# A three-layer float32 network on one core: norm weights spread by one transfer, fewer weight splits on GpSimd, and weights split earlier at the experts' end

## The chip, the core and the metric

The kernel runs on one core of a Trainium2 chip. The core has TensorE (PE, matrix products), VectorE (DVE), ScalarE (ACT), GpSimd (POOL) and SyncE (SP, which issues transfers); each takes its instructions in one fixed order and stands still while the next one waits. Transfers run on 16 DMA engines. The metric is the device time of one execution in microseconds; lower is better.

## The reference, cut to what matters

256 tokens of width 1024 go through two layers and then a second block, all in float32:

```
for i in (0, 1):
    h = gdn_mixer(x, ...) if i == 0 else s5_mixer(x, ...)    # gated delta rule / state space
    x = layer_norm(ALPHA * x + h, ln_g[i, 0], ln_b[i, 0])
    f = swiglu(x, ...) if i == 0 else moe_swiglu(x, ...)     # dense, d_ff 2816 / 8 experts, top 2
    x = layer_norm(ALPHA * x + f, ln_g[i, 1], ln_b[i, 1])
x = x + mixer(rmsnorm(x, norm_mix_g))                        # pooling and neighbourhood attention
x = x + mlp(rmsnorm(x, norm_mlp_g))                          # up, squared relu, down
out = rmsnorm(x, final_g)

layer_norm: (x - mean) * rsqrt(var + 1e-5) * g + b           # g and b have 1024 entries
```

Each weight is read from memory once.

## The kernel before

**Weights.** Every weight matrix is stored in the order of use. `load` (L310) fetches chunks of 1 MB on SyncE's queue into raw buffers `wr` (three of them, and a few more, `wx`, in the experts). A chunk holds two *pieces* of 128x1024. Each piece becomes two parts, so that the products keep float32's accuracy: `wh`, a copy by ScalarE (L290), and `wl`, the difference raw minus `wh` (L292). A product is made of three matmuls (L336 to L338: high by high, low by high, high by low). There are five buffers each for `wh` and `wl`, so at most five pieces are prepared at once; `wget` hands out the next piece and prepares those up to `self.ahead` (three) further on.

**Which engine makes `wl`.** VectorE does, except for the pieces that a stage names with `pool_splits`, which GpSimd does. Before the change GpSimd does 32 of them: 14 in the first mixer, 8 in the feed-forward, 3 in the state-space layer, 2 at the experts' end and 5 at the start of the second block.

**Norms.** A tile is 128 tokens, so there are two. `ln_part` (L848) adds the branch to the residual and takes statistics, `ln_finish` makes the deviation's inverse (L857, L365, L368, L372) and applies the norm: L868 subtracts the mean and multiplies by the gain, L870 multiplies by the inverse deviation and adds the offset. Both read `gb`, where gain and offset lie on all 128 partitions. `to_features` (L830) transposes the result on TensorE, L835 and L836 split it into two parts. `ln_rows` fills `gb` for each of the four norms of the layers, `gains` fills `gr` for the second block's: small transfers of one row each to one partition on GpSimd's queue, then one GpSimd instruction per row that spreads it over the partitions.

**Order.** The code is written in one order; side work is spawned as generators that advance as pieces of weights pass. A scheduler then decides in which order each engine gets its instructions; `issue_after` holds one instruction behind another of the same engine. So the change of one line can move neighbours too.

**The experts' end.** The last expert's second product fills two banks `pdn`; each result is split into `y1` (ScalarE) and `y2` (VectorE), scattered back to the tokens by a product `psc`, and added to `acc` (L1707). A norm with its gains follows, L1799 multiplies by the second block's gain, and TensorE transposes the outcome (`ptr`). Meanwhile TensorE runs 20 products that nothing reads (`warm`, L260).

**The first mixer's inverse.** `inverse` runs 15 dependent steps on VectorE (L610 multiply, L612 reduce), sends the result to memory (`d`) and fetches it back in another layout (`td`, eight loads on L618, half of them on SyncE's queue), and L627 goes on with it.

Of the kernel before, what the change touches and what calls it, by code (L numbers as in the profile page):

```python
# [16 lines left out]
ALU = mybir.AluOpType  # L17
# [34 lines left out]


def _cols(w, nb):
    """[K, F] -> [128, F/128/nb, nb, K/128, 128] flat per partition."""
    k, f = w.shape
    return w.reshape(k // 128, 128, f // 128, 128).transpose(1, 2, 0, 3).reshape(128, -1)


def _rows(w):  # L60
    """[K, N] -> [128, N/512, K/128, 512] flat per partition."""
    k, n = w.shape
    return w.reshape(k // 128, 128, n // 512, 512).transpose(1, 2, 0, 3).reshape(128, -1)


def _first(w):
    """The first 512 columns by rows, the others by columns."""
# [3 lines left out]
def _vec(v):  # L71
    """[K] -> [128, K/128]."""
    return v.reshape(-1, 128).T
# [5 lines left out]
def _consts():  # L79
    """Masks and index tables that the shapes alone fix, in three groups."""  # L80
# [33 lines left out]
def pack(i):  # L114
    """Device arrays from the inputs: transposes, slices and static gathers only."""
# [13 lines left out]
    # small vectors, features on partitions  # L129
# [10 lines left out]
    # FFN: w1 and w3 block by block  # L140
# [6 lines left out]
    # S5  # L147
# [14 lines left out]
    # experts  # L162
# [9 lines left out]
    # second block  # L172
# [31 lines left out]
class Kern:  # L204
# [16 lines left out]
    # -- small helpers --  # L221
# [15 lines left out]
    def spawn(self, gen, lag=0):  # L237
        """Work that runs beside the weights; it yields how many pieces of weights to let pass."""
# [15 lines left out]
    def warm(self, n):  # L254
        """Products that nothing reads, where TensorE would wait so long that its clock falls to half."""
# [7 lines left out]
    # -- weights: float32 from memory, split exactly into two float32r parts --  # L263
    def schedule(self, ap, chunks, at=0):
        """Append chunks of one weight array (lists of widths of pieces) to the order of loads."""
# [9 lines left out]
    def pool_splits(self, *ks):  # L275
        """Which of the pieces to come GpSimd splits."""
        self.on_pool.update(len(self.pieces) + k for k in ks)

    def prep(self, upto):
        """Load and split pieces as far as this one, or as the buffers reach."""  # L280
        nc = self.nc
        first = self.n_got - 1 if self.held is None else self.held
        while self.n_split <= min(upto, first + BUFS - 1, len(self.pieces) - 1):
# [5 lines left out]
            with self.tc.issue_after(self.after.ins) if self.after else nullcontext():  # L289
                nc.scalar.activation(hi[:, :w], src, AF.Copy)  # L290
# [5 lines left out]
    def load(self, c, upto=None):  # L296
        """Loads as far as the buffers reach while chunk c is in use."""
# [16 lines left out]
    def wget(self):  # L314
        """The next piece of weights (hi, lo); loads and splits run ahead of it."""
# [4 lines left out]
    def hold(self):  # L320
        """Keep the pieces from here on until they are let go."""
# [6 lines left out]
    def split(self, x1, x2, src):  # L328
        """x1 + x2 = src, both float32r."""
# [10 lines left out]
    def colblock(self, out):  # L340
        """out[f, tok] = sum over features of the next 128-column block of weights."""
# [6 lines left out]
    def rsqrt(self, pool, y, v, n):  # L348
        """y = v ** -0.5 for small tiles [128, n], Newton from an integer start."""
# [9 lines left out]
    def rsqrt1(self, y, v, mul, eps):  # L359
        """y = (mul v + eps) ** -0.5 for a few columns: a start from the table, then one Newton step."""  # L360
# [13 lines left out]
    # ------------------------------------------------------------ first layer  # L374
# [29 lines left out]
    def router(self, P):  # L404
        """The router's weights for rows that wait for their layer norm: gain in, mean out; the offset's share with the bias."""
# [15 lines left out]
    def plan_gdn(self):  # L421
        self.pool_splits(2, 5, *range(16, 24), 25, 27, 29, 31)
# [5 lines left out]
    def gdn(self):  # L428
# [4 lines left out]
        # chunks of weights that come while the buffers are full of the first ones, in the room of later matrices  # L433
# [13 lines left out]
        def gates():  # L447
            """beta and the log decays, tokens on partitions."""
# [24 lines left out]
            # log1p(e2) = ln(w) e2 / (w - 1), and e2 where w is 1  # L473
# [20 lines left out]
        def until(what, *hs):  # L494
            """Let weights pass until what comes first in the program has been put there."""
# [3 lines left out]
        # decay between every pair of tokens: segments (s0,t0) (s0,t1) (s1,t1)  # L499
# [17 lines left out]
        def project(out, base):  # L517
            """The next 128 channels: causal taps."""
# [1518 lines left out]
```

## Time and profile before

| | |
|---|---|
| median of 3 runs | 1309.83 us (1307.24 to 1312.06) |
| span of the profiled execution | 1305.7 us |
| TensorE busy | 1230.1 us, 94% of the span |
| VectorE busy | 1037.9 us, 79% |
| ScalarE busy | 732.7 us, 56% |
| GpSimd busy | 353.4 us, 27% |
| weights and other data read | 260.79 MB, 201 GB/s over the span |

The span runs from the first to the last instruction of one profiled execution; no separate time of that execution is listed, and the median of the runs shown lies 4.1 us above the span. Busy means that an instruction is in the engine; an instruction that is held by another engine's access counts as busy too, so its length has to be compared with that of its like. TensorE's busy time includes stretches at the lower of its two clock levels (1.2 instead of 2.4 GHz, shown as a granted clock of 0.50), where the same product takes about twice as long.

### The profile page before, as it was taken

To read this page: it belongs to the slowest core of one execution; us is meant where nothing else is said; L and a number is where in the kernel's file an instruction comes from. 1 tells how busy PE (TensorE), PEld (TensorE's weight loads), DVE (VectorE), ACT (ScalarE), POOL (GpSimd) and SP (SyncE) were. 2 spreads that over 40 slices of the span, in tenths; PEclk is the share of its full clock that TensorE was granted. 3 is DMA by queue.
4 is the path that set the end of the run, shared out by engine and by line. 5 is a ranking of instruction groups with operands and counts; after the bars stand their busy time and mean duration, and the time that the engine had idled before them with its cause. 6 is when DMAs were issued, how large, how long until landed. Compare 5 with 4: busy or idle time off the path is not lost. (4 is left out here: it accounts for less than half of the span.)

```text
span 1305.7 us, 19759 instructions
## 1 busy us (share of the span) xinstructions
PE 1230.1 (94%) x7579; PEld 1065.1 (82%) x7579; DVE 1037.9 (79%) x1487; ACT 732.7 (56%) x1086; POOL 353.4 (27%) x321
## 2 busy tenths in 40 slices
PE   8989997998997989899999999999999789999997
PEld 7989876997996777667888888888877677899886
DVE  6677879999865898779998989999988775766553
ACT  6635444442443544448777777767767455655442
POOL 2362014249996656223000000000003371000000
PEclk9989999899998999999999999999999899999999
DMA  8343214453651501136999889899987543455551
GB/s 324 130 138 120 85 65 151 159 188 134 227 194 65 178 33 65 57 130 217 344 343 338 326 322 373 300 333 373 335 302 293 180 151 130 166 190 187 183 189 54
DMA packets 44437, 263.46 MB, mean 202 GB/s; under 512 B 9136, under 2 KB 9536, under 8 KB 18096
## 3 DMA queue, kind: packets, MB, share of 16 engines
q1 hardware_dynamic: 40320, 257.12, 55.2%
q10 hardware_dynamic: 3472, 4.42, 1.0%
q8 instruction: 62, 1.02, 0.3%
q0 software_dynamic: 544, 0.58, 0.1%
q14 instruction: 39, 0.32, 0.1%
HBM read 260.79 MB, written 1.31 MB: 201 GB/s over the span
## 5 line engine op out<-in xcount | busy, mean ns | idle before, releaser
L292 DVE TENSOR_TENSOR wl<-wr,wh 128x1024 fp32r<-128x1024 f32 (+1 forms) x361 | 441.0, 1240 | 125.9 <-ACT wh L290 123.8
L290 ACT ACTIVATE wh<-wr 128x1024 fp32r<-128x1024 f32 (+2 forms) x390 | 391.1, 1025 | 234.4 <-PE po L338 85.8
L338 PE MATMUL pup<-wh,xg 128*128 128x512 f32 (+1 forms) x384 | 145.2, 378 | 2.7 <-PEq L1668 2.4
L337 PE MATMUL pup<-wl,xg 128*128 128x512 f32 (+1 forms) x384 | 146.3, 381 | 0.3 <-DVE wl L292 0.2
L336 PE MATMUL pup<-wh,xg 128*128 128x512 f32 (+1 forms) x384 | 145.9, 380 | 0.0
L292 DVE TENSOR_TENSOR wl<-wx,wh 128x1024 fp32r<-128x1024 f32 (+1 forms) x110 | 122.4, 1146 | 10.5 <-ACT wh L290 8.8
L290 ACT ACTIVATE wh<-wx 128x1024 fp32r<-128x1024 f32 (+1 forms) x112 | 105.0, 980 | 9.9 <-PE pup L338 5.9
L292 POOL TENSOR_TENSOR wl<-wr,wh 128x1024 fp32r<-128x1024 f32 x29 | 76.6, 2656 | 108.3 <-ACT wh L290 77.4
L338 PE MATMUL p<-x,wl 128*128 128x256 f32 x320 | 92.3, 288 | 5.5 <-DVE wl L292 5.3
L336 PE MATMUL p<-x,wh 128*128 128x256 f32 x320 | 91.7, 287 | 0.0
L337 PE MATMUL p<-x,wh 128*128 128x256 f32 x320 | 91.4, 286 | 0.0
L337 PEld LDWEIGHTS pup<-wl,xg 128*128 128x128 f32 x384 | 72.5, 189 | 14.3 <-DVE wl L292 4.0
L338 PEld LDWEIGHTS pup<-wh,xg 128*128 128x128 f32 x384 | 72.6, 189 | 14.1 <-issue 2.8
L336 PEld LDWEIGHTS pup<-wh,xg 128*128 128x128 f32 x384 | 72.8, 190 | 10.9 <-issue 0.2
L337 PE MATMUL pdn<-wl,eh 128*128 128x512 f32 x176 | 69.9, 397 | 0.0
L336 PE MATMUL pdn<-wh,eh 128*128 128x512 f32 x176 | 69.8, 397 | 0.0
L338 PE MATMUL pdn<-wh,eh 128*128 128x512 f32 x176 | 69.5, 395 | 0.0
L338 PEld LDWEIGHTS p<-x,wl 128*128 128x128 f32 x320 | 62.3, 195 | 7.0 <-DVE wl L292 6.9
L336 PE MATMUL pm<-x,wh 128*128 128x256 f32 x224 | 63.5, 283 | 0.0
L338 PE MATMUL pm<-x,wl 128*128 128x256 f32 x224 | 63.4, 283 | 0.0
L337 PE MATMUL pm<-x,wh 128*128 128x256 f32 x224 | 63.4, 283 | 0.0
L336 PEld LDWEIGHTS p<-x,wh 128*128 128x128 f32 x320 | 62.4, 195 | 0.6 <-ACT s L995 0.4
(565 smaller groups left out, 3123.2 us busy)
## 6 DMA issues: line engine op xcount, KB each, us to landing
wr<-w_e SPq DMA_DIRECT2D x59, 1024.0 KB, 6.7
wx<-w_e SPq DMA_DIRECT2D x37, 1024.0 KB, 6.7
wr<-w_f SPq DMA_DIRECT2D x33, 1024.0 KB, 4.8
wr<-w_e SPq DMA_DIRECT2D x29, 768.0 KB, 5.8
wr<-w_up SPq DMA_DIRECT2D x16, 1024.0 KB, 4.9
wr<-w_dn SPq DMA_DIRECT2D x16, 1024.0 KB, 4.9
wx<-w_e SPq DMA_DIRECT2D x19, 768.0 KB, 6.0
wr<-w_glu SPq DMA_DIRECT2D x8, 1024.0 KB, 4.7
```

Of the source, the lines that this page charges most:

```text
L290: nc.scalar.activation(hi[:, :w], src, AF.Copy)
L292: self.los[self.n_split] = eng.tensor_tensor(lo[:, :w], src, hi[:, :w], op=ALU.subtract)
L336: mm(out, lhsT=l1, rhs=r1, start=start, stop=False)
L337: mm(out, lhsT=l1, rhs=r2, start=False, stop=False)
L338: self.mm = mm(out, lhsT=l2, rhs=r1, start=False, stop=stop)
```

## The change

1. **Norm weights.** `ln_rows` and `gains` call a new function `spread`. It issues one transfer on ScalarE's queue that reads the rows once for each partition and writes all 128 (1 MB for two rows, 0.5 MB for one). The small transfers and the GpSimd spreading instructions are gone; there are six such fills.
2. **GpSimd's splits.** The lists of `pool_splits` are shortened. In the instructions as built GpSimd makes 12 differences instead of 32; the other 20 (six in the first mixer, seven in the feed-forward, three in the state-space layer, one at the experts' end, three at the second block's start) are VectorE's.
3. **The experts' end.** Before the last piece of the last expert is taken, `self.ahead` becomes four, so that one more piece of the second block is prepared; the last `y1` is issued behind the last `wh` made so far, and `y2` behind the last `wl`.

Comments and docstrings are removed too, so line numbers differ between the two files (L815 and L817 become L821; L868 and L870 become L870 and L872).

```diff
-                nc.scalar.activation(hi[:, :w], src, AF.Copy)
+                self.hi = nc.scalar.activation(hi[:, :w], src, AF.Copy)
...
     def plan_gdn(self):
-        self.pool_splits(2, 5, *range(16, 24), 25, 27, 29, 31)
+        self.pool_splits(2, 5, 16, 17, 25, 27, 29, 31)
...
     def ln_rows(self, i, pool, tag, rr=True):
         self.gb = pool.tile([128, 2, D], F32, tag=tag, name="gb")
-        for k in range(2):
-            self.nc.gpsimd.dma_start(self.gb[0:1, k, :], self.a["lnrow"][2 * i + k:2 * i + k + 1, :])
-        for k in range(2):
-            self.nc.gpsimd.partition_broadcast(self.gb[:, k, :], self.gb[0:1, k, :])
+        self.spread(self.gb, self.a["lnrow"][2 * i:2 * i + 2, :])
...
+    def spread(self, out, rows):
+        n = rows.shape[0]
+        self.nc.scalar.dma_start(out[:, :n, :], rows.partition_broadcast(128))
...
     def gains(self, i, n, pool, tag):
         g = pool.tile([128, 2, D], F32, tag=tag, name="gr")
-        for k in range(n):
-            self.nc.gpsimd.dma_start(g[0:1, k, :], self.a["rmsrow"][i + k:i + k + 1, :])
-        for k in range(n):
-            self.nc.gpsimd.partition_broadcast(g[:, k, :], g[0:1, k, :])
+        self.spread(g, self.a["rmsrow"][i:i + n, :])
...
     def plan_ffn(self):
-        self.pool_splits(0, 1, 2, 4, 6, 8, 10, 12)
+        self.pool_splits(0)
...
     def plan_s5(self):
-        self.pool_splits(0, 1, 2)
...
     def plan_moe(self):
-        self.pool_splits(36 * NE - 3, 36 * NE - 1)
+        self.pool_splits(36 * NE - 3)
...
                 for k0 in range(0, EB, 2):
+                    if (e, n) == (NE - 1, 1) and k0 + 2 >= EB:
+                        self.ahead = BUFS - 1
                     hi, lo = self.wget()
...
-                self.split(y1, y2, py)
+                with tc.issue_after(self.hi.ins) if (e, n) == (NE - 1, 1) else nullcontext():
+                    nc.scalar.activation(y1, py, AF.Copy)
+                with tc.issue_after(self.los[self.n_split - 1].ins) if (e, n) == (NE - 1, 1) else nullcontext():
+                    TT(y2, py, y1, op=ALU.subtract)
...
         self.drain()
+        self.ahead = BUFS - MO["a"]
...
     def plan_second(self):
-        self.pool_splits(0, 1, 2, 3, 4)
+        self.pool_splits(0, 2)
```

**The first place: SyncE's queue in the first mixer.** `w_go` are the mixer's output weights, `td` the inverse's result on its way back. Before:

```order
L310 DMA wr<-w_z 128x2048
L310 DMA wr<-w_q 128x2048 x4
L605 DMA d_152<-nd_146 16x16x16 x4
L310 DMA wr<-w_v 128x2048 x4
L618 DMA td<-d_153 16x16x16 x4
L310 DMA wr<-w_go 128x2048 x4
L310 DMA wr<-w_f 128x2048 x33
```

and in the changed kernel:

```order
L310 DMA wr<-w_z 128x2048
L310 DMA wr<-w_q 128x2048 x4
L605 DMA d_152<-nd_146 16x16x16 x4
L310 DMA wr<-w_v 128x2048 x4
L310 DMA wr<-w_go 128x2048
L618 DMA td<-d_153 16x16x16 x4
L310 DMA wr<-w_go 128x2048 x3
L310 DMA wr<-w_f 128x2048 x33
```

The first chunk of `w_go` now stands ahead of the four loads of `td`.

**The second place: VectorE between the feed-forward and the state-space layer.** The rows begin at the first tile's norm (`lnr` holds the sums, `gb` the gain and offset, `x` the normed rows; `x_71<-ptr` is the low part of the transposed rows). Before:

```order
L868 SCALAR_TENSOR_TENSOR lnr<-lnr,lnmv,gb 128x512 x2
L848 SCALAR_TENSOR_TENSOR lnr<-x,po 128x512
L368 SCALAR_TENSOR_TENSOR rs_4585<-lnrs,rs_4583 128x1
L849 BN_STATS lnst<-lnr 128x6
L372 SCALAR_TENSOR_TENSOR lnrs<-rs_4585,lnrs 128x1
L870 SCALAR_TENSOR_TENSOR x<-lnr,lnrs,gb 128x512 x2
L848 SCALAR_TENSOR_TENSOR lnr<-x,po 128x512
L292 TENSOR_TENSOR wl<-wr,wh 128x1024
L836 TENSOR_TENSOR x_71<-ptr,x_70 128x4x128 x2
L849 BN_STATS lnst<-lnr 128x6
L292 TENSOR_TENSOR wl<-wr,wh 128x1024
L857 BN_AGGR lnmv<-lnst 128x2
```

and in the changed kernel:

```order
L870 SCALAR_TENSOR_TENSOR lnr<-lnr,lnmv,gb 128x512 x2
L850 SCALAR_TENSOR_TENSOR lnr<-x,po 128x512
L368 SCALAR_TENSOR_TENSOR rs_4579<-lnrs,rs_4577 128x1
L851 BN_STATS lnst<-lnr 128x6
L372 SCALAR_TENSOR_TENSOR lnrs<-rs_4579,lnrs 128x1
L292 TENSOR_TENSOR wl<-wr,wh 128x1024
L872 SCALAR_TENSOR_TENSOR x<-lnr,lnrs,gb 128x512 x2
L850 SCALAR_TENSOR_TENSOR lnr<-x,po 128x512
L292 TENSOR_TENSOR wl<-wr,wh 128x1024
L838 TENSOR_TENSOR x_71<-ptr,x_70 128x4x128 x2
L851 BN_STATS lnst<-lnr 128x6
L292 TENSOR_TENSOR wl<-wr,wh 128x1024
```

A split of weights (L292) now stands ahead of the normed rows `x`, a second one ahead of the transposed rows' low part, and a third directly behind the second tile's statistics.

**The third place: VectorE at the experts' end.** `y` from `pdn` is the low part of the last result, `acc<-psc` the last sum, `lnst` the norm's statistics. Before:

```order
L331 TENSOR_TENSOR y_14731<-pdn,y_14730 128x512
L292 TENSOR_TENSOR wl<-wx,wh 128x1024
L1632 SCALAR_TENSOR_TENSOR acc<-psc,rgate,acc 128x512 x2
L292 TENSOR_TENSOR wl<-wx,wh 128x1024
L1698 BN_STATS lnst<-acc 128x6 x2
L331 TENSOR_TENSOR y_14803<-pdn,y_14802 128x512
L1707 SCALAR_TENSOR_TENSOR acc<-psc,rgate,acc 128x512
L1708 BN_STATS lnst<-acc 128x6
L857 BN_AGGR lnmv<-lnst 128x2
L365 TENSOR_SCALAR rs_14850<-lnmv 128x1
```

and in the changed kernel:

```order
L1685 TENSOR_TENSOR y_14719<-pdn,y_14718 128x512
L292 TENSOR_TENSOR wl<-wx,wh 128x1024
L1630 SCALAR_TENSOR_TENSOR acc<-psc,rgate,acc 128x512 x2
L292 TENSOR_TENSOR wl<-wx,wh 128x1024
L292 TENSOR_TENSOR wl<-wx,wh 128x512
L1703 BN_STATS lnst<-acc 128x6 x2
L292 TENSOR_TENSOR wl<-wr,wh 128x1024 x2
L1685 TENSOR_TENSOR y_14795<-pdn,y_14794 128x512
L292 TENSOR_TENSOR wl<-wr,wh 128x1024
L1712 SCALAR_TENSOR_TENSOR acc<-psc,rgate,acc 128x512
L1713 BN_STATS lnst<-acc 128x6
L859 BN_AGGR lnmv<-lnst 128x2
```

Ahead of the last `y` there are three more splits (one of 128x512), and a fourth stands between it and the last sum.

## Rows read from the trace of the kernel before

**Rows 1.** The page's first two parts: span; busy time, share, instructions of each engine.
```profile
span 1305.7 us, 19759 instructions
...
PE 1230.1 (94%) x7579; PEld 1065.1 (82%) x7579; DVE 1037.9 (79%) x1487; ACT 732.7 (56%) x1086; POOL 353.4 (27%) x321
```

**Rows 2.** Waits of TensorE: who waits for whom, us in all, times, longest.
```profile
PE ptn L954 <- DVE s L981: 5.8, 1, 5.8
```

**Rows 3.** Windows: busy us of PE, PEld, DVE, ACT, POOL; clock; DMA share; GB/s.
```profile
80.00:100.00 20.00, 16.69 (x117) 16.48 (x116) 19.45 (x45) 8.76 (x16) 8.55 (x4) 0.83 0.46 159
225.00:325.00 100.00, 90.14 (x652) 85.88 (x653) 99.67 (x169) 38.40 (x54) 54.86 (x51) 0.97 0.45 153
405.00:425.00 20.00, 11.01 (x51) 9.92 (x50) 11.67 (x17) 6.47 (x9) 7.51 (x7) 0.74 0.00 0
425.00:435.00 10.00, 7.48 (x34) 5.17 (x34) 9.67 (x11) 1.14 (x3) 7.94 (x5) 1.00 0.59 211
600.00:1000.00 400.00, 397.27 (x1888) 333.95 (x1887) 362.21 (x386) 296.03 (x358) 7.60 (x4) 1.00 0.91 335
1010.00:1030.00 20.00, 13.13 (x50) 9.10 (x50) 19.10 (x31) 7.42 (x16) 8.67 (x4) 0.74 0.30 105
```

**Rows 4.** The page's costliest groups: the weight splits of VectorE.
```profile
L292 DVE TENSOR_TENSOR wl<-wr,wh 128x1024 fp32r<-128x1024 f32 (+1 forms) x361 | 441.0, 1240 | 125.9 <-ACT wh L290 123.8
```

**Rows 5.** Line 610 by source; then timelines of GpSimd and SyncE in the first mixer.
```profile
L610 DVE TENSOR_TENSOR pr<-tt,nd x15: 172/410/2144, 79.5 to 98.7; 128x1 f32<-128x1 f32 x1, 128x4 f32<-128x4 f32 x1, 128x9 f32<-128x9 f32 x1, 128x16 f32<-128x16 f32 x1
...
90.17 2.36 POOL L292 TENSOR_TENSOR wl<-wr,wh 128x1024 fp32r<-128x1024 f32 x1 [3.67 <-ACT wh L290]
...
102.87 5.35 SPq L618 DMA_DIRECT2D td<-d  x4
...
109.47 0.35 SPq L310 DMA_DIRECT2D wr<-w_go  x1
```

**Rows 6.** Timeline of VectorE from the first mixer's end into the feed-forward.
```profile
198.83 3.53 DVE L870 SCALAR_TENSOR_TENSOR x<-lnr,lnrs,gb 128x512 f32<-128x512 f32 x2
...
220.93 5.20 DVE L1134 TENSOR_SCALAR SS<-SS 128x64 f32<-128x64 f32 x5
...
232.23 3.39 DVE L292 TENSOR_TENSOR wl<-wr,wh 128x1024 fp32r<-128x1024 f32 x1
```

**Rows 7.** Timelines between feed-forward and state-space layer: GpSimd, then VectorE, then TensorE.
```profile
412.54 2.48 POOL L817 PARTITION_BROADCAST gb<-gb  x2 [5.82 <-issue]
...
413.87 2.21 DVE L868 SCALAR_TENSOR_TENSOR lnr<-lnr,lnmv,gb 128x512 f32<-128x512 f32 x2 [8.05 <-POOL gb L817]
...
427.84 2.32 DVE L368 SCALAR_TENSOR_TENSOR rs<-lnrs,rs 128x1 f32<-128x1 f32 x1
...
418.37 1.12 PE L830 MATMUL ptr<-cg,x 128*128 128x128 f32 x4 [8.99 <-DVE x L870]
...
434.06 1.32 PE L830 MATMUL ptr<-cg,x 128*128 128x128 f32 x8 [1.07 <-DVE x L870]
```

**Rows 8.** Timelines at the experts' end: GpSimd, then VectorE, then TensorE.
```profile
1006.60 12.07 POOL L292 TENSOR_TENSOR wl<-wr,wh 128x1024 fp32r<-128x1024 f32 x5
...
1008.64 0.69 DVE L331 TENSOR_TENSOR y<-pdn,y 128x512 fp32r<-128x512 f32 x1 [1.98 <-ACT y L330]
...
1009.92 0.75 DVE L1707 SCALAR_TENSOR_TENSOR acc<-psc,rgate,acc 128x512 f32<-128x512 f32 x1 [0.59 <-PE psc L1625]
...
1014.09 2.29 DVE L368 SCALAR_TENSOR_TENSOR rs<-lnrs,rs 128x1 f32<-128x1 f32 x1
...
1026.38 0.21 DVE L368 SCALAR_TENSOR_TENSOR rs<-lnrs,rs 128x1 f32<-128x1 f32 x1
...
1021.42 1.94 PE L830 MATMUL ptr<-cg,xn 128*128 128x128 f32 x8 [6.87 <-DVE xn L1799]
...
1030.72 1.03 PE L830 MATMUL ptr<-cg,xn 128*128 128x128 f32 x8
```

**Rows 9.** The page's transfers: a 1 MB weight chunk, KB, us to landing.
```profile
wr<-w_f SPq DMA_DIRECT2D x33, 1024.0 KB, 4.8
```

## The prediction

> **What bounds the kernel now.** The page's first two parts come first: TensorE is busy for 94% of 1305.7 us, VectorE for 79%, GpSimd for 27% [rows 1]. So about 75 us at most can be won from TensorE's idle time, and the question is where that time lies. The windows answer it. In the experts (600 to 1000 us) TensorE works 397.27 of 400 us; nothing is to be had there. From 405 to 425 us it works 11.01 of 20, from 1010 to 1030 us 13.13 of 20, from 80 to 100 us 16.69 of 20, and in the feed-forward's first 100 us 90.14, while VectorE is full there (99.67) [rows 3]. In the three short windows the granted clock is 0.74, 0.74 and 0.83, so TensorE spent part of them at 1.2 GHz after it had stood idle. The waits and the timelines then say who was waited for. At 418.37 us `ptr` had waited 8.99 us for the normed rows, whose norm stood 8.05 us for `gb` from GpSimd [rows 7]. At 1021.42 us `ptr` had waited 6.87 us for `xn` [rows 8]. In the feed-forward `ptn` waited 5.8 us for `s` [rows 2].
>
> The second thing to see is a length. The same small operation of VectorE, line 368, takes 2.32 us at 427.84, 2.29 us at 1014.09 and 0.21 us at 1026.38 [rows 7, 8]. The long ones lie beside a GpSimd split (five of those fill 1006.60 to 1018.67, 2.41 us each [rows 8]), the short one beside none. So a split on GpSimd isn't free for VectorE: one that meets a VectorE operation of this kind costs it about 2.1 us. On VectorE the split itself costs 1.24 us [rows 4].
>
> **Part by part.** The sum goes by the place where TensorE waits, in us gained.
>
> *The feed-forward's end.* GpSimd spreads `gb` at 412.54 to 415.02, late because its own work precedes it; line 868 starts at 413.87 and had been idle for 8.05, so it could have begun at 405.82 [rows 7]. The new transfer reads its rows long before: it stands in ScalarE's queue ahead of the last groups of the feed-forward, and a 1 MB transfer takes 4.8 us to land [rows 9]. From line 868's start to `ptr` are 4.50 us (413.87 to 418.37). In the new order one split, 1.24 us, stands ahead of `x`. So `ptr` comes at 405.82 + 4.50 + 1.24 = 411.6, 6.8 us earlier. What follows shrinks too. The second tile's `ptr` stands at 434.06, 15.7 us behind the first. Of those, TensorE idled 2.5 (425 to 435: 7.48 of 10 busy). A clock of 0.74 over 20 us means 10.4 us at half rate; 9 of the 20 were idle, so about 5 fell on work and cost 2.5 [rows 3]. Without both it is 10.7 us; the three splits that VectorE takes over here (3.7 us) about match the holds that go. I take 11: second `ptr` at 422.6, a gain of 11.5. Bounds: 7 if the 15.7 us stay as they are, 13 if the split ahead of `x` falls into idle time as well.
>
> *The experts' end.* Three more splits, one of them half size, now stand ahead of the last `y`, a fourth ahead of the last sum: 3.5 x 1.24 = 4.3 us. VectorE idled 1.98 and 0.59 us just there, so 1.7 us remain, and the sum starts at 1011.6 instead of 1009.92 [rows 8]. From it to `ptr` were 11.50 us. Three operations in between (868, 368, 372) are held by GpSimd's five splits, 2.1 us each by the row of 368: 6.2 us. GpSimd now has two of those five, which end about 1011.4 (1006.60 + 2 x 2.41), before these operations. That makes 11.5 - 6.2 = 5.3 us and `ptr` at 1016.9, 4.5 earlier. The low clock (again 10.4 us of 20, some 5 on work) may add up to 2.5 us, but the second tile's chain behind it doesn't shrink alike; I take 5, bounds 2 (all four splits on the path) and 8 (low clock gone, splits hidden).
>
> *The first mixer.* Six splits add 7.4 us to VectorE between 74 and 100 us. Four of line 610's steps take about 2 us (longest 2.144) where the shortest takes 0.172 [rows 5]: about 7.4 us are given back. VectorE was busy 19.45 of 20 us and stays so. TensorE's 3.3 us of idle time and the low clock (0.83: 6.8 us at half rate, 3.4 lost) are the most to be won, 6.7. Against it stands SyncE's queue: the first `w_go` chunk, issued at 109.47, now stands ahead of `td`, whose loads went out from 102.87 to 108.22 [rows 5]. `w_go` waits for a raw buffer that the last splits of queries free; if it waits as before, `td` starts 6.9 us later and ends at least 3 us later, and the inverse with it. I take 1, bounds -5 and 6.7.
>
> *Into the feed-forward.* Seven splits are 8.7 us more on a VectorE that is full. Three rows show what goes: two operations of line 870 took 3.53, where one of that shape takes 0.75; five tiny ones of line 1134 took 5.20 (0.21 each would be 1); a split took 3.39 instead of 1.24 [rows 6, 8, 4]. Together 2.0 + 4.2 + 2.15 = 8.4. I take 0. Bounds: 9, if the wait for `s` (5.8) goes and the low clock with it (0.97 over 100 us: 3 lost), and -4, if half of the holds would have been in VectorE's idle time.
>
> *What costs nothing.* Six issues on ScalarE at about 0.35 us (as SyncE's `w_go` [rows 5]); ScalarE is busy 56%, and its slack covers them (2 us if not). In the experts two fills put 1.5 MB on the transfer engines, 4.5 us at 335 GB/s; with a DMA share of 0.91, 36 of 400 us are free [rows 3]. I take 0, bounds -4.5 and 0. The spreads at the other norms are off the chain; the split of the experts' last piece is counted above.
>
> The sum is 11.5 + 5 + 1 + 0 = 17.5 us.
>
> At one point a rule speaks for more. The Trainium skill, "SBUF — State Buffer", section "Who interferes with whom", says that a VectorE instruction with two SBUF inputs and a GpSimd instruction that reads SBUF exclude each other, and the later one is blocked until the first ends. The rows of line 368 agree. By the rule alone each of the 20 splits could free its whole 2.41 us, which less 20 x 1.24 would be 23 us, and with the wait for `gb` the time would be near 1279.
>
> **Rivals.** (a) *More*: TensorE gets the whole of its idle time and low clock in the mixer and the feed-forward. 11.5 + 5 + 6.7 + 9 = 32, time 1278. For it speaks that each hold ends with its GpSimd split; against it, that VectorE, full in both stretches, carries 16 us more of splits. (b) *Given back*: `td` behind `w_go` takes 5, the gains at the two ends stay at 7 and 2: 4 us, time 1306. For it: SyncE's new order. Against: TensorE has projections to work on meanwhile. (c) *Slower*, by VectorE's queue: a split on VectorE waits for its `wh`, and everything behind it in the queue waits too. On GpSimd such a wait was harmless: 3.67 us at 90.17 [rows 5]. If the thirteen splits of mixer and feed-forward wait w each, 13 w is lost: at w = 1.4 the gain is gone, at 1.9 the kernel is slower by over 0.5%, at 2.5 the time is 1310 - 17.5 + 32.5 = 1325. Against it: VectorE's idle time before all its splits is 125.9 us for 361, 0.35 each [rows 4]. (d) *Not what it says*: ScalarE reaches the fill too late, since the transfer stands behind an activation that waits, or waits itself for the room that `gb` takes over. Then the norm stands as long as before and only the other terms hold: 6 us, time 1304. It would take a delay of some 80 us between the tables' end and 405.
>
> One more sentence of the notes bears on the fills: the Trainium skill, "DMA: Bandwidth & Descriptors", section "Issuing engines are not separate DMA queues", says that transfers share the same 16 engines whichever queue issues them. If the experts' stream had no slack, that would make it 4.5 us longer, as in the bound above; no row shows a wait for a chunk there.
>
> **How the numbers follow.** The sum stands against the profiled span, 1305.7, which lies 4.1 us below the median of the runs, 1309.83; I carry that difference over. The forecast is 1309.8 - 17.5 = 1292 (span 1288), its own range 1285 to 1298, with a chance of 0.54; (a) 0.19, (b) 0.14, (c) 0.06, (d) 0.07. About 0.5%, 6.5 us, is what a measurement of this kernel can tell from no change. The forecast, (a) and four tenths each of (b) and (d) make 0.81 for faster; the rest of (b) and (d) make 0.13 for the same, (c) 0.06 for slower. The range reaches into (a) to 1274 and takes half of (b) and (d), to 1305.
>
> **What would show it.** Right: `gb` filled before 405; line 868 following line 365 without a wait; first `ptr` there about 7 us earlier than 418 when counted from the last `po` product, and no clock at 0.50 behind it; line 368 at 0.2 us at the experts' end and the wait for `xn` below 4 us; VectorE's splits without growing idle time before them. Wrong: a wait of the norm for `gb`; TensorE waiting for `pT` or a `py` of the inverse near 110 us, with `td` issued after `w_go`; VectorE's waits for `wh` in the mixer; a longer stretch from 225 to 325. The prediction fails if the mixer's or the feed-forward's stretch changes by more than its bounds, above all if the splits' order, not their length, decides.

## The result and the profile after

The changed kernel takes 1287.55 us (median of 4 runs, 1283.21 to 1291.15), the kernel before 1309.3 in the same comparison; the ratio is 0.9829, with a 95% interval from 0.9807 to 0.9851. The forecast was 1292. The page of the profiled execution, to be held against [rows 1]:

```profile
span 1285.3 us, 19687 instructions
...
PE 1229.9 (96%) x7579; PEld 1062.8 (83%) x7579; DVE 1031.8 (80%) x1507; ACT 732.3 (57%) x1086; POOL 280.1 (22%) x279
```

TensorE's busy time is the same; 20.4 us of span are gone, and TensorE's idle time went down by as much. That execution took 1287.1 us, 1.8 us above its span. In windows (as in [rows 3]: busy time of PE, PEld, DVE, ACT and POOL, granted clock, DMA share, GB/s) the stretches that answer to 225, 405 and 1010 us of before are:

```profile
220.00:320.00 100.00, 90.73 (x662) 85.66 (x662) 98.29 (x177) 40.09 (x57) 45.71 (x48) 0.98 0.47 169
402.00:422.00 20.00, 19.19 (x97) 16.27 (x96) 18.30 (x31) 10.46 (x16) 6.05 (x6) 1.00 0.37 132
996.00:1016.00 20.00, 16.66 (x68) 10.11 (x68) 18.15 (x38) 8.07 (x19) 0.81 (x2) 0.83 0.28 105
```

TensorE now works 19.19 of the 20 us in which it worked 11.01, at full clock. At the experts' end it works 16.66 of 20 instead of 13.13, part of it still at the lower clock. Two of its waits now, by who waits for whom (us in all, times, longest):

```profile
PE ptn L953 <- DVE lnr L850: 2.3, 1, 2.3
PE ptn L953 <- DVE s L980: 2.1, 1, 2.1
```

The wait for `xn` (6.9) is gone and the wait for `s` fell from 5.8 to 2.1 [rows 2]; the wait for `lnr` is new, and so are waits of 2.9 us for `y` and 1.9 for `Tm` (their rows are in experiments 8 and 4).

To see where the time went, the span can be cut at products that both kernels have in the same place of TensorE's order, and each stage measured in TensorE's timeline. All stages add up to the span (us):

| stage, up to | before | changed | spread alone | lists alone |
|---|---|---|---|---|
| second tile's `ptr` behind the first mixer | 210.22 | 209.78 | 209.95 | 211.93 |
| end of the feed-forward's last `po` | 199.16 | 196.24 | 198.83 | 197.54 |
| second tile's `ptr` for the state-space layer | 24.68 | 11.76 | 17.30 | 21.30 |
| first `pup` of the experts | 159.51 | 161.22 | 161.39 | 159.86 |
| end of the last `pdn` | 414.40 | 415.72 | 414.02 | 415.34 |
| second tile's `ptr` for the second block | 22.75 | 19.30 | 21.57 | 18.28 |
| end | 274.95 | 271.32 | 271.75 | 274.99 |

The last two columns are the first two experiments below. One caution for reading such a table: two profiles of the changed kernel agree within 0.4 us in five stages, and differ in the two where their clocks differ. The second profile has 208.26 for the first stage (209.78 above), with a granted clock of 1.00 from 112 to 130 us instead of 0.81, and 195.51 for the second (196.24), with 1.00 from 220 to 240 us instead of 0.91. So steps up to some 1.6 us between two profiles, where a stretch at 1.2 GHz falls or doesn't, say nothing about an edit.

### The profile page after: what moved, and what is told of

Read it like the earlier page. It is cut to its first block, busy times and chain, and to the rows that moved or that the text cites. A ratio compares the mean times of both kernels' runs of the same rounds, so it can differ in the third digit from the quotient of the medians.

```text
span 1285.3 us, 19687 instructions
## 1 busy us (share of the span) xinstructions
PE 1229.9 (96%) x7579; PEld 1062.8 (83%) x7579; DVE 1031.8 (80%) x1507; ACT 732.3 (57%) x1086; POOL 280.1 (22%) x279
## 5 line engine op out<-in xcount | busy, mean ns | idle before, releaser
L292 DVE TENSOR_TENSOR wl<-wr,wh 128x1024 fp32r<-128x1024 f32 (+1 forms) x380 | 461.7, 1233 | 131.3 <-ACT wh L290 129.3
L292 DVE TENSOR_TENSOR wl<-wx,wh 128x1024 fp32r<-128x1024 f32 (+2 forms) x111 | 124.3, 1153 | 10.6 <-ACT wh L290 9.1
L292 POOL TENSOR_TENSOR wl<-wx,wh 128x1024 fp32r<-128x1024 f32 x1 | 2.5, 2478 | 409.8 <-ACT wh L290 409.8
```

The source lines that it names most:

```text
L292: self.los[self.n_split] = eng.tensor_tensor(lo[:, :w], src, hi[:, :w], op=ALU.subtract)
```

## The experiments

**1. The new transfer alone, and the shorter lists alone.** The kernel before with `spread` in place of the GpSimd fills:

```diff
     def ln_rows(self, i, pool, tag, rr=True):
-        ... two transfers and two partition_broadcast on GpSimd
+        self.spread(self.gb, self.a["lnrow"][2 * i:2 * i + 2, :])
     def gains(self, i, n, pool, tag):
-        ... n transfers and n partition_broadcast on GpSimd
+        self.spread(g, self.a["rmsrow"][i:i + n, :])
```

Expected:

> The kernel before with the one change that gain and offset rows are spread by one transfer on ScalarE's queue; GpSimd keeps its 32 splits. Theory (the late fill of gb is what the feed-forward's end costs): the wait of 8.99 us for the normed rows falls below 2 us, the mixer of the second block is about 3 us shorter, the experts' end keeps its 6.9 us wait; in all 10 to 14 us less than before, about 1297. Rival (GpSimd's splits hold VectorE there in any case): at most 4 us less, 1305 to 1309.

The kernel before with the new lists of `pool_splits` and nothing else:

```diff
-        self.pool_splits(2, 5, *range(16, 24), 25, 27, 29, 31)
+        self.pool_splits(2, 5, 16, 17, 25, 27, 29, 31)
...
-        self.pool_splits(0, 1, 2, 4, 6, 8, 10, 12)
+        self.pool_splits(0)
...
-        self.pool_splits(0, 1, 2)
...
-        self.pool_splits(36 * NE - 3, 36 * NE - 1)
+        self.pool_splits(36 * NE - 3)
...
-        self.pool_splits(0, 1, 2, 3, 4)
+        self.pool_splits(0, 2)
```

Expected:

> The kernel before with only the shorter lists of GpSimd splits (12 instead of 32). Theory: the wait for gb stays at about 9 us; the feed-forward gains 3, the state-space layer's start 3, the experts' end 4, the first mixer 0; about 1300. Rival (VectorE is full, and what is taken from GpSimd is paid there): no gain, 1308 or more.

Measured: 1296.58 us (ratio 0.99, 0.9886 to 0.9913) for the transfer, 1301.02 us (0.9938, 0.9923 to 0.9952) for the lists. Both theories hold in size, 13 and 9 us less; the rivals of both fall. The sum of the two, 22, is as much as the whole change. TensorE's waits of the two kernels say how they differ, first the transfer alone:

```profile
PE ptr L832 <- DVE xn L1798: 6.9, 1, 6.9
PE ptr L832 <- DVE x L872: 6.7, 2, 5.1
```

and the lists alone:

```profile
PE ptr L830 <- DVE x L870: 11.2, 2, 9.0
...
PE ptr L830 <- DVE xn L1798: 0.6, 1, 0.6
```

With the transfer alone the longest wait for the normed rows is 5.1 us, not below 2 as expected, and the experts' end still waits 6.9. With the lists alone it is the other way round: the norm still waits 9.0 for `gb`, and the wait for `xn` is down to 0.6. At the feed-forward's end (third stage) the two give 7.4 and 3.4 us alone and 12.9 together: each takes away a wait behind which the other's stood. The last stage is the transfer's alone (271.75 against 274.95, the 3 us expected), most of the gain at the experts' end the lists'. Two parts of the lists' forecast missed: the feed-forward gains 1.6 us and not 3, and the first mixer, expected at 0, takes 1.7 longer.

**2. The state-space layer's list back.** The changed kernel, with GpSimd making that layer's first three splits:

```diff
     def plan_s5(self):
+        self.pool_splits(0, 1, 2)
```

Expected:

> The changed kernel with the state-space layer's list as before, so GpSimd makes its first three splits. Theory (the fill brings the first tile's rows early, the three splits hold the second tile's norm): the first tile's transposes as early as in the changed kernel, the second tile's 2 us later behind them, 12 instead of 10; about 2 us more in all. Rival (the fill alone did it): no change.

Measured: 1291.31 us (0.9863, 0.9846 to 0.9881), against 1287.55 and 1285.97 for the changed kernel. The third stage is 17.70 us, 5.9 more, of which only 2.5 lie between the tiles. So the theory had the cause and not the place: it is the first tile that is held. In GpSimd's timeline of this kernel, and then in VectorE's (start, us, engine, line, operation):

```profile
402.36 2.40 POOL L292 TENSOR_TENSOR wl<-wr,wh 128x1024 fp32r<-128x1024 f32 x1
405.41 5.07 POOL L292 TENSOR_TENSOR wl<-wr,wh 128x1024 fp32r<-128x1024 f32 x2 [0.65 <-ACT wh L290]
```

```profile
402.58 3.39 DVE L870 SCALAR_TENSOR_TENSOR lnr<-lnr,lnmv,gb 128x512 f32<-128x512 f32 x2
...
406.49 1.71 DVE L368 SCALAR_TENSOR_TENSOR rs<-lnrs,rs 128x1 f32<-128x1 f32 x1
...
408.72 1.78 DVE L372 SCALAR_TENSOR_TENSOR lnrs<-rs,lnrs 128x1 f32<-128x1 f32 x1
```

Two operations of line 870 that take 0.75 each elsewhere take 3.39 together, and lines 368 and 372, on one column each, 1.71 and 1.78: these two end at 408.20 and 410.50, with GpSimd's second and third split (408.18 and 410.48). The changed kernel has none of these splits; its VectorE timeline at the same place:

```profile
402.30 0.15 DVE L365 TENSOR_SCALAR rs<-lnmv 128x1 f32<-128x1 f32 x1
402.38 1.94 DVE L870 SCALAR_TENSOR_TENSOR lnr<-lnr,lnmv,gb 128x512 f32<-128x512 f32 x2
...
404.83 0.21 DVE L368 SCALAR_TENSOR_TENSOR rs<-lnrs,rs 128x1 f32<-128x1 f32 x1
...
405.57 0.14 DVE L372 SCALAR_TENSOR_TENSOR lnrs<-rs,lnrs 128x1 f32<-128x1 f32 x1
405.63 1.21 DVE L292 TENSOR_TENSOR wl<-wr,wh 128x1024 fp32r<-128x1024 f32 x1
406.76 1.40 DVE L872 SCALAR_TENSOR_TENSOR x<-lnr,lnrs,gb 128x512 f32<-128x512 f32 x2
```

and TensorE's:

```profile
407.70 0.60 PE L832 MATMUL ptr<-cg,x 128*128 128x128 f32 x4
...
417.78 1.32 PE L832 MATMUL ptr<-cg,x 128*128 128x128 f32 x8 [0.80 <-DVE x L872]
```

Line 870 starts 0.08 us after line 365 has started: `gb` lies ready (its transfer, issued at 314.41, had landed at 318.95). The split ahead of `x` (1.21) is there as the order had it; with GpSimd's splits back it isn't. The three lines are 1.45, 1.50 and 1.64 us longer there, 4.6 in all; less the split that is 3.4, which is what the first `ptr` is later (5.12 us behind the last `po` instead of 1.68). The 2.5 us between the tiles aren't the second tile's norm: TensorE is busy for all 12.57 us between the two `ptr`, with ten products that the changed kernel does ahead of the first, and at a clock of 0.78 instead of 1.00.

**3. The feed-forward's list back.** The changed kernel with the seven splits on GpSimd again:

```diff
     def plan_ffn(self):
-        self.pool_splits(0)
+        self.pool_splits(0, 1, 2, 4, 6, 8, 10, 12)
```

Expected:

> The changed kernel with the feed-forward's list as before, so GpSimd makes seven splits there again. Theory (each held VectorE's table work longer than a split takes it): the wait of ptn for s rises from 2 towards 6 us, and 2 to 3 us more than the changed kernel in all, about 1288.5. Rival (VectorE is full there and pays the splits back): no change.

Measured: 1289.53 us (0.9846, 0.9826 to 0.9866). The second stage is 199.49 us, 3.3 more than the changed kernel's 196.24 (4.0 more than its other profile's 195.51), and the wait for `s` is back:

```profile
PE ptn L953 <- DVE s L980: 5.7, 1, 5.7
```

So the seven splits are worth 3 to 4 us there, although VectorE is full in the changed kernel too (98.29 of 100 us): on balance they freed more of its time than they take. The rival falls in this stage. The whole time doesn't show it as clearly: the medians are 2.0 and 3.6 us apart with intervals that overlap, and this profile's span, 1284.1 us, is no longer than the changed kernel's, since its stages one and five, which this edit doesn't touch, happen to be shorter (207.40 and 413.80). Why they are is open.

**4. The first mixer's list back.** The changed kernel with the six splits of the queries on GpSimd:

```diff
-        self.pool_splits(2, 5, 16, 17, 25, 27, 29, 31)
+        self.pool_splits(2, 5, *range(16, 24), 25, 27, 29, 31)
```

Expected:

> The changed kernel with the first mixer's list as before, so GpSimd makes the six splits of the queries again. Theory (what TensorE gains in the projections is lost again at the inverse): the wait before the query norms comes back, 3 us, and the wait before the inverse's first transpose goes; in all within 2 us of the changed kernel. Rival (the six splits are worth their holds): 4 to 6 us more than the changed kernel, about 1293.

Measured: 1284.65 us (0.9812, 0.9799 to 0.9826), 2.9 us below the first and 1.3 below the second measurement of the changed kernel (next), with overlapping intervals. The first stage is 209.44 us beside 209.78 and 208.26. So the six splits bring nothing either way. Both halves of the theory hold: the wait before the query norms is 3.31 us again (1.05 in the changed kernel), and `pT` comes without a wait, at 111.38. How the changed kernel loses it is seen in its profile. VectorE, between and at the last steps of the inverse:

```profile
94.94 1.21 DVE L292 TENSOR_TENSOR wl<-wr,wh 128x1024 fp32r<-128x1024 f32 x1
...
102.17 2.58 DVE L610 TENSOR_TENSOR pr<-tt,nd 128x225 f32<-128x225 f32 x1
...
104.78 0.39 DVE L612 TENSOR_REDUCE tt<-pr 128x15 f32<-128x225 f32 x1
...
113.56 1.63 DVE L627 TENSOR_TENSOR Tm<-td,cg 128x512 f32<-128x512 f32 x2 [1.00 <-DMA td<-d]
```

SyncE's queue, which had `w_go` put ahead of `td`:

```profile
106.38 0.33 SPq L310 DMA_DIRECT2D wr<-w_go  x1
107.00 4.95 SPq L618 DMA_DIRECT2D td<-d  x4
```

and TensorE's wait there:

```profile
114.74 0.63 PE L633 MATMUL pT<-cg,Tm 128*128 128x128 f32 x4 [1.94 <-DVE Tm L627]
```

TensorE is 4.7 us ahead of before at 93 us (the product at 98.01 there is at 93.32 here). But the inverse's last step ends at 105.2, where it ended at 100.0 before. Of these 5.2 us, 3.3 are there ahead of its first step, because its input `nd`, which comes back from memory too, lands late. ScalarE's queue, SyncE's queue and VectorE before:

```profile
77.54 0.35 ACTq L606 DMA_DIRECT2D nd<-d  x1
...
79.11 13.78 SPq L310 DMA_DIRECT2D wr<-w_v  x3
...
79.54 1.93 DVE L610 TENSOR_TENSOR pr<-tt,nd 128x1 f32<-128x1 f32 x1 [7.10 <-DMA nd<-d]
```

and in the changed kernel:

```profile
77.49 21.28 SPq L310 DMA_DIRECT2D wr<-w_v  x4
...
77.91 0.35 ACTq L606 DMA_DIRECT2D nd<-d  x1
...
82.80 0.16 DVE L610 TENSOR_TENSOR pr<-tt,nd 128x1 f32<-128x1 f32 x1 [2.87 <-DMA nd<-d]
```

The first 1 MB chunk of `w_v` waits for a raw buffer that a split of the queries frees. Before, GpSimd made that split; VectorE makes it 1.6 us sooner, so the chunk goes out 0.4 us ahead of `nd` instead of 1.6 us behind it, and `nd` (128 KB) lands 4.9 us after its issue instead of 2.0. All thirteen profiles agree: `nd` takes 4.8 or 4.9 us in the nine with the shorter mixer's list, where the chunk goes first, and 2.0 or 2.1 in the four with the old one (before, the transfer alone, this experiment and the last of experiment 9), where `nd` does. The other 1.9 us are lost between the steps: four splits of the queries stand there instead of one, and one that GpSimd still has (101.93 to 104.34) holds line 610 for 2.58 us. `pT` comes at 114.74 instead of 110.94, and behind it a stretch at half clock (116 to 123 us in this profile). `w_go` isn't the cause: `td` went out at 107.00, as soon as the result had landed in memory (sent at 105.20, 1.7 us to landing), and so did ScalarE's half of it, which has no weights ahead of it.

**5. The changed kernel again.** Expected:

> The changed kernel itself once more, beside the three below on the same chip, so that differences of 3 us can be read. All theories expect 1285 to 1289; a median below 1285.5 would mean that the two kernels with 1284.65 (without the third part, and with the first mixer's list as before) are no faster than the changed one.

Measured: 1285.97 us (1284.93 to 1291.61; 0.9827, 0.9804 to 0.9849). With the first four the nine runs have a median of 1286.1. So it stands only 0.5 above the stated 1285.5: by the medians alone, the two kernels with 1284.65 can't be told from the changed one.

**6. The second block's gains as before.** The changed kernel, where only `gains` goes back to GpSimd:

```diff
     def gains(self, i, n, pool, tag):
-        self.spread(g, self.a["rmsrow"][i:i + n, :])
+        for k in range(n):
+            self.nc.gpsimd.dma_start(g[0:1, k, :], self.a["rmsrow"][i + k:i + k + 1, :])
+        for k in range(n):
+            self.nc.gpsimd.partition_broadcast(g[:, k, :], g[0:1, k, :])
```

Expected:

> The changed kernel with the second block's gains filled as before (small transfers, then GpSimd spreads them); the layers' norms keep the new transfer. Theory (the 3 us won inside the second block's mixer come from this fill, since GpSimd's spreading and the waits around it delay its window sums): the waits for the scores come back, 2 to 3 us more than the changed kernel, about 1290. Rival (they come from the new order of the products that the other edits bring): no change.

Measured: 1290.93 us (0.9863, 0.9843 to 0.9882), 5.0 more than the changed kernel beside it. The last stage is 275.82 us, 4.1 to 4.5 more. GpSimd's timeline of this kernel:

```profile
1013.15 1.21 POOL L947 DMA_DIRECT2D gr<-rmsrow  x2
1023.60 2.48 POOL L949 PARTITION_BROADCAST gr<-gr  x2 [9.23 <-issue]
1033.52 1.63 POOL L1965 TENSOR_TENSOR w<-u 128x256 f32<-128x256 f32 x2 [7.45 <-issue]
```

and of the changed one:

```profile
1029.22 1.21 POOL L1962 TENSOR_TENSOR w<-u 128x256 f32<-128x256 f32 x2 [12.85 <-ACT u L1984]
```

Between the issue of the two rows (1013.15) and GpSimd's next work (1033.52) lie 20 us, of which only 2.48 are spreading; 9.23 and 7.45 are idle, with no releaser that the profile shows. Counted from the second tile's `ptr` (1010.86 here, 1014.02 in the changed kernel) the window sums (line 1965 here, 1962 there) start 22.7 us later with the fill and 15.2 without it. GpSimd's sums and its scaling of the scores (`Pr`) are then late; ScalarE waits 7.03 us for the scaling (0.24 in the changed kernel), and TensorE for the scores behind it, which it doesn't in the changed kernel:

```profile
1044.39 0.51 ACT L1928 ACTIVATE Pr<-s,m 128x256 f32<-128x256 f32 x1 [7.03 <-POOL Pr L1931]
...
1049.95 1.09 PE L1918 MATMUL psc<-k,q 64*128 64x256 f32 x4 [2.94 <-DVE s L1921]
```

The theory holds, with a loss above the 2 to 3 us expected, and the rival (no change) falls.

**7. The selection behind the norm.** In the changed kernel a selection of the experts (`Sel`) had moved ahead of the second tile's norm. The edit puts it back:

```diff
-        nc.vector.bn_stats(st[:, n[0], :], r)
+        self.stat = nc.vector.bn_stats(st[:, n[0], :], r)
...
-                r = TT(Sel[:, t, es], ...)
+                with tc.issue_after(self.stat.ins) if es.start == 0 else nullcontext():
+                    r = TT(Sel[:, t, es], ...)
```

Expected:

> The changed kernel with one order put back: the experts' first selection (1.5 us of VectorE) stands behind the second tile's statistics again, as in the kernel before. Theory (that selection ahead of the norm makes TensorE wait 2.3 us and lowers its clock, the 2 us lost ahead of the experts): 1.5 to 2.5 us less than the changed kernel. Rival (the selection is late then, or the clock falls anyway): no change or up to 1 us more.

VectorE's timeline in the changed kernel:

```profile
563.95 1.50 DVE L1540 TENSOR_TENSOR Sel<-cg,rpos 128x256 fp32r<-128x256 f32 x1
...
565.82 1.03 DVE L850 SCALAR_TENSOR_TENSOR lnr<-x,sg 128x256 f32<-128x256 f32 x1
```

TensorE waited 2.27 us for that `lnr`, and the clock was at half from 567 to 574. With the edit:

```profile
562.88 0.44 PE L953 MATMUL ptn<-cg,lnr 128*128 128x128 f32 x2 [0.85 <-DVE lnr L850]
```

The wait is 0.85 us. Measured: 1283.99 us (0.9806, 0.9788 to 0.9824), 2.0 less than the changed kernel beside it. The fourth stage is 156.49 us in this profile, 4.7 less; 1.6 of that are a stretch of low clock near 525 us that this profile lacks, and the two kernels of experiment 9, with the same edit, have 1.8 less in this stage. The other 1.3 lie behind that norm, where this profile is at full clock and the first kernel of experiment 9 isn't (1.00 and 0.87 from 566 to 574 us). The intervals overlap, so the stage carries the verdict, not the medians. The kernel with the transfer alone has the long stage already (161.39), the one with the lists alone hasn't: the transfer brought the new order.

**8. Without the third part.** The changed kernel with the experts' end as before:

```diff
-                    if (e, n) == (NE - 1, 1) and k0 + 2 >= EB:
-                        self.ahead = BUFS - 1
...
-                with tc.issue_after(self.hi.ins) ...: nc.scalar.activation(y1, py, AF.Copy)
-                with tc.issue_after(self.los[self.n_split - 1].ins) ...: TT(y2, py, y1, op=ALU.subtract)
+                self.split(y1, y2, py)
```

Expected:

> The changed kernel without its third part: no further piece prepared ahead of the last product, and the last result split without being held behind the next weights. Theory (the splits put ahead of the last sum cost more than they give): the last sum starts 3 us earlier, the norm behind it is as short as in the changed kernel; 2 to 4 us less than the changed kernel, about 1285. Rival (the splits then stand inside the norm and the first products wait for them): 2 to 4 us more than the changed kernel, about 1291.

Measured: 1284.65 us (0.9807, 0.9794 to 0.982). The sixth stage is 17.96 us, 1.3 to 1.4 less than the changed kernel's 19.30 and 19.40. In the changed kernel VectorE and then TensorE read, from the last splits on:

```profile
995.05 3.33 DVE L292 TENSOR_TENSOR wl<-wr,wh 128x1024 fp32r<-128x1024 f32 x2
998.31 0.68 DVE L1685 TENSOR_TENSOR y<-pdn,y 128x512 fp32r<-128x512 f32 x1
998.91 1.21 DVE L292 TENSOR_TENSOR wl<-wr,wh 128x1024 fp32r<-128x1024 f32 x1
1000.04 0.74 DVE L1712 SCALAR_TENSOR_TENSOR acc<-psc,rgate,acc 128x512 f32<-128x512 f32 x1
...
1002.52 0.21 DVE L368 SCALAR_TENSOR_TENSOR rs<-lnrs,rs 128x1 f32<-128x1 f32 x1
```

```profile
999.04 1.22 PE L1623 MATMUL psc<-y,SelT 128*128 128x512 f32 x2 [2.90 <-DVE y L1685]
1000.19 6.26 PE L260 MATMUL warm<-zero 128*64 128x512 bf16 x20
1006.51 1.10 PE L832 MATMUL ptr<-cg,xn 128*128 128x128 f32 x8
```

The last `pdn` ended at 994.72, `y` followed only at 998.31, and TensorE waited 2.90 us for it; then its 20 products that nothing reads (`warm`, 6.26 us, partly at half clock) ended at 1006.45, when `xn` was complete already (1006.11): `ptr` no longer waited for it. Without the third part VectorE has:

```profile
995.07 0.68 DVE L331 TENSOR_TENSOR y<-pdn,y 128x512 fp32r<-128x512 f32 x1
996.33 0.75 DVE L1706 SCALAR_TENSOR_TENSOR acc<-psc,rgate,acc 128x512 f32<-128x512 f32 x1 [0.59 <-PE psc L1623]
...
997.73 1.21 DVE L292 TENSOR_TENSOR wl<-wr,wh 128x1024 fp32r<-128x1024 f32 x1
...
999.82 1.22 DVE L292 TENSOR_TENSOR wl<-wr,wh 128x1024 fp32r<-128x1024 f32 x1
```

`y` comes 1.46 us after the last `pdn` (993.61), not 3.59. Two splits now lie inside the norm (997.73 and 999.82), which is what the rival said, and `ptr` waits 1.5 us for `xn`; but that is less than the wait for `y` was. The direction of the theory holds, with 1.3 to 1.4 us in the stage where 2 to 4 were expected.

**9. Together.** The changed kernel with the edits of experiments 7 and 8:

Expected:

> The changed kernel with two orders put back: the experts' first selection behind the second tile's statistics, and no third part (the last result is split ahead of the next weights). The two lie at different places: 3 to 4 us less than the changed kernel, 1282 to 1283. If one of the two gains was chance, 1284 to 1285.

Measured: 1283.16 us (1281.96 to 1284.01; 0.9794, 0.9781 to 0.9808), 4.4 and 2.8 us less than the changed kernel's two medians; stages four and six are 159.39 and 18.26. It has the lowest median of all kernels here; its interval lies below that of before by far and overlaps the changed kernel's by a little. An earlier run has the edit of experiment 4 on top of them:

Expected:

> The changed kernel without its third part, with the first mixer's list as before, and with the selection behind the norm. If the three are separate places, 5 to 8 us less than the changed kernel, 1280 to 1283; if two of the differences were chance, 2 to 3 us less.

Measured: 1283.95 us (0.9798, 0.9783 to 0.9814): no further gain, 2 us less than the changed kernel beside it. The three differences don't add up to the 5 expected at least; by the expectation's own words two of them would be chance. The stages say one: the fourth and the sixth are as short as above (159.37 and 18.26), and the first (209.63) is no shorter than the changed kernel's, so the mixer's list is the one without a gain.

## Why the forecast came out right, and where not

The total was right: 17.5 us forecast, 21.8 measured in the medians and 20.4 in the two profiled spans, and the largest term had the right cause. That the total is so close is in part chance, since the terms missed in both directions. By terms (the profiles' stages, before less changed):

| term | forecast | measured |
|---|---|---|
| feed-forward's end | 11.5 | 12.9 |
| experts' end | 5 | 3.45, less 1.3 in the stage ahead |
| first mixer | 1 | 0.4 |
| into the feed-forward | 0 | 2.9 |
| ahead of the experts | not named | -1.7 |
| second block | 0 ("off the chain") | 3.6 |

*The feed-forward's end.* The mechanism and both halves are shown: the first `ptr` comes 1.68 us behind the last `po` instead of 8.99 (7.3 won, 6.8 forecast), and the second follows after 10.1 us (11 forecast). Where the forecast put the three removed splits at nothing ("about match the holds that go"), they are worth 5.9 us by experiment 2: with `gb` there early, GpSimd's splits would have stood beside the first tile's norm and held it, where they stood behind it before. The 1.2 us of the split ahead of `x` cost little, because TensorE does ten products of its own there (1.8 us) that stood between the two `ptr` before.

*The experts' end* was over-sized: 2.1 in all. The holds went as forecast (line 368 takes 0.21 us, GpSimd ends at 996.2), and from the sum the norm runs without a wait (line 368 at 1002.52, 2.48 us behind it). The step that failed is "so 1.7 us remain": the last sum starts 5.3 us after the last `pdn`, where it started 1.95 after it, so 3.4 remain. The two splits ahead of `y` took 3.33 us instead of 2.4, since the first of them was held until GpSimd's remaining two ended at 996.2 (five in [rows 8]). The last piece's split came late too, for which the last `pdn` waited 0.8 us; this comes from the list, since the kernel of experiment 8 has the same wait without the third part. And `ptr` came 6.5 us behind the sum where 5.3 were forecast: `xn` took 6.1 of them, and the rest went to the products of `warm`, which the forecast didn't count.

*The first mixer* came out as forecast for another reason. TensorE did win the 4.7 us in the projections. It lost them at the inverse, and the forecast had the right danger at the wrong transfer: not `td` behind `w_go`, but `nd` behind `w_v`, which starts the inverse 3.3 us later (experiment 4). It looked only at the place where the order of issue differs; at the other a chunk went out earlier because its buffer came free earlier. Between the steps 1.9 us more were lost: of the 7.4 us that line 610 was to give back, 3.7 came (its 15 steps take 8.1 us instead of 11.8), and the splits put between the steps took more.

*Into the feed-forward* the forecast's step "I take 0" was too careful: 2.9 us, and experiment 3 shows 3 to 4, while the lists alone gave 1.6. VectorE stays full; the wait for `s` falls from 5.8 to 2.1, inside the stated bounds (-4 to 9).

*What costs nothing.* Here a step was wrong: "The spreads at the other norms are off the chain." The second block's is not; by experiment 6 its fill costs 4 to 5 us, because it keeps GpSimd from work for 20 us while TensorE's scores wait for GpSimd. And the new order ahead of the experts, which no edit names, cost some 2 us (experiment 7).

Rival (a) asked for everything in mixer and feed-forward: a part came, in the feed-forward. (b) came true at the experts' end, and in the first mixer in kind, at `nd`. (c) did not: VectorE's idle time before its splits is 131.3 us for 380, 0.35 each as before, and between the inverse's steps no split waited for its `wh`; three ahead of them waited 3.4 us in all, while `nd` was not there anyhow. (d) is excluded by line 870, which no longer waits. The Trainium skill's rule ("SBUF — State Buffer", section "Who interferes with whom": the later of two such instructions is blocked until the first ends) agrees with experiment 2, where lines 368 and 372 end with GpSimd's splits. But the 23 us that the forecast worked out by it for the splits are far above what they gave: 8.7 us for all 20 when the lists alone are changed.

## What to carry to other kernels

A helper engine's time isn't free where it shares something with the busy one: compare the same small instruction beside the helper's work and away from it, and count that difference as the price. Before calling an engine's small job hidden, look at how long that engine is out of work around it, not at the job's own length. After a change that a scheduler spreads, compare the orders at places no edit touches: here one moved instruction cost some 2 us, and putting it back gave them again. And where a buffer is freed sooner, look at what goes out sooner with it: here a 1 MB chunk got ahead of a small transfer that a chain of dependent steps waited for, and cost it 3 us.

## What the runs showed of the hardware that was not expected

The fill through GpSimd took it out for 20 us for 2.48 us of spreading (9.23 and 7.45 us idle without a releaser in the profile, 5.82 at the feed-forward's end [rows 7]). In the trace two instructions that change GpSimd's configuration stand ahead of the spreading (1014.60 and 1014.64 in experiment 6) and two behind it (1025.99 and 1026.02); the idle time follows each pair. The Trainium skill, "GPSIMD Engine Reference", section "2.1 Instruction dispatch", says that the first call of freshly loaded code on GpSimd pays about 6 us without a visible instruction; the gaps here agree in kind, and they come on the way back too, where 7.45 us are a quarter longer. In the 9.23 us ahead a second wait is hidden: the two small transfers landed 5.8 and 6.0 us after their issue, the last at 1019.7, so only 3.9 us lie behind the landing. With the transfer on ScalarE's queue, which lands in 4.5 to 7.7 us for 1 MB (median 4.8 in the layers' norms) and 4.5 for 0.5 MB, nothing of this is left. A transfer of 128 KB that was issued 0.4 us behind a 1 MB chunk of another engine's queue took 4.9 us to land instead of 2.0 (experiment 4). Two profiles of one and the same program differ by 1.5 us in a stage, where a stretch at a granted clock of 0.50 follows a wait in one and not in the other (behind 114 us: 0.81 against 1.00 from 112 to 130 us). What sets that apart stays open here.
